# Two-layer RWKV-7 / short-convolution trunk: the triangular inverse of a chunk, in blocks of 48 or of 24

## The chip, the cores and the metric

The kernel runs on one core of one Trainium2 chip. The metric is device time in microseconds (us), from the first to the last instruction of the program with the little that lies around it; lower is better. One launch does the whole step: a prompt of 512 positions with 16 meta tokens ahead of it (528 positions), and 8 sample positions, 536 columns in all.

## The reference, cut to what matters

Each of the two layers is a half-step feed-forward block (FFN), a mixer, and a second half-step FFN. The mixer projects the normalised input, and its costly part is the RWKV-7 recurrence, for each of 16 heads of 64 channels, over the 528 prompt positions:

```
def _wkv_step(S, inp):
    r_t, w_t, k_t, v_t, a_t, b_t = inp
    Sa = jnp.einsum('bhvk,bhk->bhv', S, a_t)
    S = S * w_t[:, :, None, :] + Sa[..., None] * b_t[:, :, None, :] + v_t[..., None] * k_t[:, :, None, :]
    y = jnp.einsum('bhvk,bhk->bhv', S, r_t)
    return S, y
...
    seq_in = tuple(jnp.moveaxis(t, 1, 0) for t in (rh, wh, kh, vh, -kk, kk * ah))
    S_T, y = lax.scan(_wkv_step, wkv0.astype(f32), seq_in)
```

The state S of a head is updated with its own product with a_t, so the positions of a chunk depend on each other through a triangular system. The rest of the mixer is a group norm of y, a bonus term, a short convolution, two sigmoid gates and the product with W_o.

## The kernel before, in words

**Mixer.** The 16 heads go in 8 pairs p, two heads of 64 channels side by side on 128 partitions. The 528 positions are cut into NC = 11 chunks of C = 48. For each pair there are four pieces of code, all in the function `mixer`:

- `stage_k(p)` projects k and r, builds decay products, and fills `BK` and `mv` (operands whose products, `wg` on TensorE, are the 48x48 matrices of a chunk, for two heads 96x96 rows and columns). Its masked strictly triangular part is the tile `GT`, the other part `GR`. Then comes the inverse, (1 - G)^-1 of each chunk and head, 22 small triangular matrices of 48x48 for a pair.
- `stage_v(p)` projects v and makes `P1`, what a chunk contributes without the state.
- `chain(p)` runs through the 11 chunks in order. Each chunk takes the state `sd`, and goes TensorE (`cq<-mv,sd`), VectorE (`rh`), TensorE (transpose), VectorE (`rd`), TensorE with the inverse as weights (`cq<-rd,Yd`), ScalarE (`ud`), TensorE (`cq<-GR,ud`), VectorE (`sx`), TensorE (transpose), VectorE (`sd`). `cq` is one bank of PSUM, tag `c0` or `c1` by p % 2.
- `gnorm(p)` normalises the outputs of the pair, on the same bank.

Between them `fill` puts parts of the convolution and gate work (`gated_parts`), which depend on nothing in the chain. `sample()`, near the end of a mixer, does the recurrence for the 8 sample positions, with a good part of its elementwise work on GpSimd.

**The inverse.** `GT` is stored to DRAM (`td<-GT`), and read back so that each of 88 partitions holds a matrix: 22 matrices, four times (`Ta` its first 24 rows, `Tb` the rest). Partition group q works on the rows j of X with j % 4 = q. X starts as the identity (`Xinv<-in_xid`, a DMA). Then 47 steps, column by column: a product (`pr<-Ta,Xinv`) and an addition (`Xinv<-Xinv,pr`), both on GpSimd, since no pair is listed in `inv`. X is stored (`xd<-Xinv`, four DMAs), and read back in the layout of TensorE's weights (`Yd<-xd`, two DMAs), into one of two buffers `yds[p % 2]`. `Xinv`, `Ta`, `Tb` and `pr` have one buffer each.

**What sets the order.** Nothing is issued as it is written. `Sched.add` records every operation (so all instructions have the line of `issue`, L268, and are told apart by their tiles), and `flush` replays them as a list scheduler: it takes the operation that is ready and has the best priority (`prio`, its place less `boost`; the table `MIX` has the boosts by kind of work), and advances its own clocks by `price`. Each engine then runs its instructions strictly in that order, and so does the one DMA queue, SyncE's. The prices thus fix the order; how long things take is the chip's matter. The table `MIX`, with the fills in `gated`, is the same in both kernels. Small operations of GpSimd (`NS`, `SGA`, `GSs`, `MBs`, `CVP`, `pe`, copies of a few columns) stand in its order between the steps of the inverse; some of them are the last readers of tiles that other engines then write anew.

In `price`, times are in us and n is the number of elements of a partition:

```
return (max(n, 256) / 2400 + (12e-3 if self.ffn else 2.3e-3) if ins[0].dtype == F32R else n / 600 + 6e-3), self.HOP
...
last = any(tuple(x.ap[-1])[0] == 0 for x in ins)
return 0.155 + n * (1.63e-3 if last else 2.07e-3), self.HOP
```

The first is TensorE's, the last two GpSimd's, in a mixer. Matrix products in a mixer are mostly `acc`, projections in three fp32r products of 268 columns a block (`hi` and `lo` are the weights split by ScalarE and VectorE, from `raw`, the weights as loaded by SyncE's queue).

Of the kernel before, what the change touches and what calls it, by code (L numbers as in the profile page):

```python
# [15 lines left out]
P = 128  # L16
# [16 lines left out]
NC = L // C  # L33
D = 64
# [62 lines left out]
class Sched:  # L97
# [41 lines left out]
    def price(self, eng, fn, out, ins, kw):  # L139
        n = self.width(out)  # L140
        if fn == "dma_start":
            return 0.48, 4 * n * out.shape[0] / self.DMA_RATE
        if eng == "tensor":
            if fn == "transpose" or kw.get("is_transpose"):
                return n / 1200 + 2e-3, self.HOP
            return (max(n, 256) / 2400 + (12e-3 if self.ffn else 2.3e-3) if ins[0].dtype == F32R else n / 600 + 6e-3), self.HOP
        if eng == "vector":
            if fn == "memset":
                return 8e-3 + n / 960, self.HOP
            if fn == "reciprocal":  # L150
# [3 lines left out]
            return (0.13 if len(ins) > 2 else 0.07) + n / 960, self.HOP  # L154
        if eng == "scalar":
            psum = any(x.tensor.space == PSUM for x in ins + [out])
            return (0.05 if psum else 0.095) + (0.09 if "scale" in kw else 0) + n / 1200, self.HOP
        if self.ffn:
            return 0.1 + n * 3.1e-3, self.HOP
        last = any(tuple(x.ap[-1])[0] == 0 for x in ins)  # L160
        return 0.155 + n * (1.63e-3 if last else 2.07e-3), self.HOP

    def add(self, eng, fn, args, kw):
# [7 lines left out]
        if eng == "tensor":  # L171
            o.cols0 = (o.cost - 2.3e-3) * 2400
            o.cols = o.cols0 * ins[0].shape[0] / 128
# [165 lines left out]
def v2(ap):  # L339
    return ap.rearrange("p (a b) -> p a b", a=2)  # L340

# [5 lines left out]
class Build:  # L347
# [425 lines left out]
    def mixer(self, l, xh, xl, mD):  # L773
# [8 lines left out]
        with ExitStack() as ctx:  # L782
# [86 lines left out]
            def shift(i, acc, out, sample=None, dup=False):  # L869
                ps = tmp("ps_")  # L870
                V.memset(ps[:, 0:1], 0.0)
                evict(ps[:, 1:1 + NT], acc)
                G.tensor_copy(out=NS[:, i, :], in_=ps[:, L:L + 1 + NB])
                t = tmp("t_")
                n = NT if sample is not None else L
                A.activation(out=t[:, :n], in_=ps[:, 1:1 + n], func=AF.Copy, scale=omu[:, i:i + 1])
                pv, tv = ps[:, 0:L], t[:, :L]
                if dup:
                    pv, tv = c3(pv), c3(tv)
# [43 lines left out]
            def stage_k(p):  # L923
# [58 lines left out]
                for h in range(2):  # L982
                    hs = slice(h * D, (h + 1) * D)
                    V.scalar_tensor_tensor(out=BK[hs, :, h * C:(h + 1) * C], in0=c3(ka[hs, :L]), scalar=pc("kk", p)[hs],
                                           in1=c3(rn[hs, :L]), op0=ALU.mult, op1=ALU.mult)
# [30 lines left out]
                HC = C // 2  # L1016
                Ta = pp.tile([P, HC, C], F32, tag="Ta", name="Ta")
                Tb = pp.tile([P, HC, HC], F32, name="Tb")
                tdv = td.rearrange("h c s t -> (h c) s t")
                for q in range(4):  # L1020
                    S.dma_start(out=Ta[q * 22:(q + 1) * 22], in_=tdv[:, :HC, :])
                    S.dma_start(out=Tb[q * 22:(q + 1) * 22], in_=tdv[:, HC:, HC:])
                NP = 88
                nc.boost = boost['i']
                X = pp.tile([P, C // 4, C], F32, name="Xinv")
                pr = pp.tile([P, 176], F32, name="pr")
                I = V if p in opt['inv'] else G
                S.dma_start(out=X[:NP].rearrange("p j t -> p (j t)"), in_=io["xid"])
                for st in range(C - 1):
                    nj, nt = st // 4 + 1, C - 1 - st  # L1030
                    tr = Ta[:NP, st, st + 1:] if st < HC else Tb[:NP, st - HC, st - HC + 1:]
                    pv = pr[:NP, :nj * nt].rearrange("p (j t) -> p j t", j=nj)
                    I.tensor_tensor(out=pv, in0=tr.unsqueeze(1).to_broadcast([NP, nj, nt]),
                                    in1=X[:NP, :nj, st:st + 1].to_broadcast([NP, nj, nt]), op=ALU.mult)
                    I.tensor_tensor(out=X[:NP, :nj, st + 1:], in0=X[:NP, :nj, st + 1:], in1=pv, op=ALU.add)
                xd = dd.tile([2, NC, C, C], F32, tag="xd", name="xd")
                for q in range(4):
# [22 lines left out]
            def stage_v(p):  # L1060
# [3 lines left out]
                for h in range(2):  # L1064
                    hs = slice(h * D, (h + 1) * D)
                    V.tensor_copy(out=BK[hs, :, h * C:(h + 1) * C], in_=c3(s["kt"][hs, :]))
                v = pp.tile([P, NC, 2, C], F32, name="v")
# [4 lines left out]
                for cs in PCS:  # L1072
                    n = len(cs)
                    w = psp.tile([P, 512], F32, tag="wk", name="wv")
                    for i, c in enumerate(cs):
                        T.transpose(w[:2 * C, i * P:(i + 1) * P], v[:, c].rearrange("p a t -> p (a t)"), cst["id"])
# [15 lines left out]
                E('bv').tensor_tensor(out=c3(bv), in0=c3(s["rs"]), in1=v[:, :, 0, :], op=ALU.mult)  # L1092
                s["bv"] = bv

            def chain(p):
# [5 lines left out]
                for c in range(NC):  # L1101
                    o1, o2, o3 = order(c)
                    cq = psp.tile([P, 512], F32, tag=tg, name="cq", bufs=1)
                    rh = pp.tile([P, 2, C], F32, tag="rh", name="rh", bufs=2)
                    pb = P1[:, c, o1:o1 + C].unsqueeze(1).to_broadcast([P, 2, C])
                    if sd is not None:
                        T.matmul(out=cq[:, :QW], lhsT=sd, rhs=mvc(mv, c), start=True, stop=True)
                        V.tensor_tensor(out=rh, in0=cq[:, o1:o1 + C].unsqueeze(1).to_broadcast([P, 2, C]), in1=pb, op=ALU.add)
# [4 lines left out]
                    T.matmul(ct[:2 * C, 0:P], rh.rearrange("p a t -> p (a t)"), cst["id"], is_transpose=True, **gc)  # L1113
# [122 lines left out]
            def sample():  # L1236
# [233 lines left out]
def _consts():  # L1470
# [11 lines left out]
    s = np.arange(P) % C  # L1482
# [5 lines left out]
    o["mv"] = ((np.arange(P) // C)[:, None] == hb[None]).astype(f)  # L1488
# [4 lines left out]
def _xid():  # L1493
    import numpy as np
    x = np.zeros((88, C // 4, C), np.float32)
    for p in range(88):
        for j in range(C // 4):
            x[p, j, 4 * j + p // 22] = 1
# [82 lines left out]
```

## Time and profile before

| what | value |
|---|---|
| median of 3 runs | 3038.67 us (3034.83 to 3040.36) |
| the profiled execution | 3028.59 us, span 3026.8 us |
| mean granted TensorE clock | 0.973 |
| TensorE busy | 2835.8 us, 94% of the span |
| VectorE, ScalarE, GpSimd busy | 2170.7, 1337.4, 1043.2 us |
| GpSimd in the steps of the inverse | 402.0 + 200.0 + 166.0 us |

The first mixer lies from about 394 to 1115 us of the span, the second from 1893 to 2615; the rest is FFN, and there GpSimd is all but idle. In the rows of the profile, "idle before" is the time for which an engine stood still ahead of an instruction, and the arrow names what ended the wait. A matrix product of fp32 operands is two MATMUL instructions, one of fp32r or a transpose is one. TensorE's granted clock is 1.0 or 0.5 in stretches of 3.41 us.

### The profile page before, as it was taken

To read this page: it belongs to the slowest core of one execution; us is meant where nothing else is said; L and a number is where in the kernel's file an instruction comes from. 1 tells how busy PE (TensorE), PEld (TensorE's weight loads), DVE (VectorE), ACT (ScalarE), POOL (GpSimd) and SP (SyncE) were. 2 spreads that over 40 slices of the span, in tenths; PEclk is the share of its full clock that TensorE was granted. 3 is DMA by queue.
4 is the path that set the end of the run, shared out by engine and by line. 5 is a ranking of instruction groups with operands and counts; after the bars stand their busy time and mean duration, and the time that the engine had idled before them with its cause. 6 is when DMAs were issued, how large, how long until landed. Compare 5 with 4: busy or idle time off the path is not lost. (4 is left out here: it accounts for less than half of the span.)

```text
span 3026.8 us, 56336 instructions
## 1 busy us (share of the span) xinstructions
PE 2835.8 (94%) x22146; PEld 2782.0 (92%) x22146; DVE 2170.7 (72%) x3995; ACT 1337.4 (44%) x2190; POOL 1043.2 (34%) x1886
## 2 busy tenths in 40 slices
PE   8999998988997899999999999999898988899997
PEld 8999998988897889999999999888888888899997
DVE  8777676766775868776687776766777659687774
ACT  5444453433443345444444444534444332554444
POOL 1000037776777811000100001477877778100001
PEclk9999999999999999999999999999999999999999
DMA  4233333223323462333323323332233133623232
GB/s 134 90 102 98 116 97 83 69 84 89 94 63 91 149 199 91 96 97 102 108 77 92 102 89 126 89 82 72 82 97 94 46 113 130 209 88 98 95 105 78
DMA packets 203802, 303.88 MB, mean 100 GB/s; under 512 B 102704, under 2 KB 110256, under 8 KB 203536
## 3 DMA queue, kind: packets, MB, share of 16 engines
q1 hardware_dynamic: 203536, 300.27, 32.7%
q8 instruction: 174, 2.85, 0.4%
q14 instruction: 92, 0.75, 0.1%
HBM read 264.49 MB, written 35.72 MB: 99 GB/s over the span
## 5 line engine op out<-in xcount | busy, mean ns | idle before, releaser
L268 ACT ACTIVATE hi<-raw 128x1024 fp32r<-128x1024 f32 (+4 forms) x460 | 387.4, 845 | 498.3 <-PE acc L268 188.9
L268 DVE TENSOR_TENSOR lo<-raw,hi 128x1024 fp32r<-128x1024 f32 (+4 forms) x460 | 461.0, 1004 | 78.6 <-ACT hi L268 71.8
L268 PE MATMUL acc<-xh,lo 128*128 128x268 f32 (+1 forms) x2112 | 484.5, 303 | 15.6 <-DVE lo L268 15.4
L268 PE MATMUL acc<-xh,hi 128*128 128x268 f32 (+1 forms) x2112 | 484.9, 304 | 11.4 <-ACT hi L268 4.8
L268 PE MATMUL acc<-xl,hi 128*128 128x268 f32 (+1 forms) x2112 | 482.3, 301 | 0.0
L268 POOL MEMSET wide<- 128x104 f32 (+1 forms) x7 | 1.3, 188 | 1328.7 <-DVE lo L268 1264.1
L268 POOL TENSOR_TENSOR Xinv<-Xinv,pr 88x140 f32<-88x140 f32 (+36 forms) x752 | 402.0, 535 | 54.8
L268 PEld LDWEIGHTS acc<-xh,lo 128*128 128x128 f32 x2112 | 350.2, 195 | 19.7 <-DVE lo L268 19.4
L268 PEld LDWEIGHTS acc<-xh,hi 128*128 128x128 f32 x2112 | 350.8, 195 | 16.8 <-ACT hi L268 8.3
L268 PEld LDWEIGHTS acc<-xl,hi 128*128 128x128 f32 x2112 | 348.4, 195 | 0.2
L268 PE MATMUL a<-hh,lo 128*128 128x268 f32 (+1 forms) x1408 | 287.6, 286 | 0.2 <-DVE lo L268 0.2
L268 PE MATMUL a<-hl,hi 128*128 128x268 f32 (+1 forms) x1408 | 287.2, 285 | 0.0
L268 PE MATMUL a<-hh,hi 128*128 128x268 f32 (+1 forms) x1408 | 286.5, 285 | 0.0
L268 POOL TENSOR_TENSOR pr<-Ta,Xinv 88x150 f32<-88x150 f32 (+21 forms) x384 | 200.0, 521 | 147.9 <-DMA Xinv<-in_xid 57.5
L268 PE MATMUL x<-xh,hi 128*128 128x268 f32 (+1 forms) x864 | 247.1, 286 | 1.6 <-ACT sn L268 1.6
L268 PE MATMUL x<-xl,hi 128*128 128x268 f32 (+1 forms) x864 | 247.0, 286 | 0.0
L268 PE MATMUL x<-xh,lo 128*128 128x268 f32 (+1 forms) x864 | 246.8, 286 | 0.0
L268 ACT ACTIVATE hi<-s 128x1024 fp32r<-128x1024 f32 x144 | 151.3, 1057 | 177.1 <-DVE s L268 101.3
L268 PEld LDWEIGHTS a<-hh,lo 128*128 128x128 f32 x1408 | 219.3, 188 | 0.5 <-DVE lo L268 0.4
L268 PEld LDWEIGHTS a<-hl,hi 128*128 128x128 f32 x1408 | 218.6, 188 | 0.0
L268 PEld LDWEIGHTS a<-hh,hi 128*128 128x128 f32 x1408 | 218.5, 188 | 0.0
L268 DVE TENSOR_TENSOR lo<-s,hi 128x1024 fp32r<-128x1024 f32 x144 | 173.4, 1221 | 16.5 <-ACT hi L268 15.7
(562 smaller groups left out, 7235.2 us busy)
## 6 DMA issues: line engine op xcount, KB each, us to landing
raw<-in_f_in SPq DMA_DIRECT2D x176, 512.0 KB
raw<-in_w_in SPq DMA_DIRECT2D x132, 512.0 KB
raw<-in_f_out SPq DMA_DIRECT2D x128, 256.0 KB
raw<-in_f_out SPq DMA_DIRECT2D x32, 384.0 KB
raw<-in_w_o SPq DMA_DIRECT2D x32, 256.0 KB
Ta<-td SPq DMA_DIRECT2D x64, 99.0 KB
XD<-X SPq DMA_DIRECT2D x16, 268.0 KB
s<-in_swkv SPq DMA_DIRECT2D x16, 256.0 KB
```

The costliest lines, as they stand in the source:

```text
L268: return getattr(getattr(self.nc, o.eng), o.fn)(*o.args, **o.kw)
```

## The change

The 48x48 matrix of a chunk and head is taken as two diagonal blocks of HC = 24 and one block off the diagonal. GpSimd inverts only the diagonal blocks, 44 of 24x24 for a pair: 88 partitions hold 44 matrices twice, group q does the rows with j % 2 = q, and there are 23 steps. The block off the diagonal is the product of the lower inverse, the block itself and the upper inverse, made on TensorE, in two groups of 6 and 5 chunks: a transpose (`w1`), a product (`w2`), a product (`w3`), each followed by a copy out of PSUM on ScalarE (`x1`, `x2`, and into `Yd`). They use the chain's bank `c{p % 2}`. The rows of a chunk for the two heads are interleaved by blocks (head 0 and 1 of the first half, then of the second), so the views of `BK`, `v`, `rh`, the masks and `mv` change with it (`g3` where `c3` stood), with the same numbers of elements. `Ta` and `Xinv` have two buffers; `Tb` is gone.

```
-            return (max(n, 256) / 2400 + (12e-3 if self.ffn else 2.3e-3) if ins[0].dtype == F32R else n / 600 + 6e-3), self.HOP
+            return (max(n, 256) / 2400 + 12e-3 if ins[0].dtype == F32R else n / 600 + 6e-3), self.HOP
...
+            if not self.ffn and len(ins) > 1 and all(x.tensor.space != PSUM for x in ins):
+                return fixed + n / 860, self.HOP
...
-        last = any(tuple(x.ap[-1])[0] == 0 for x in ins)
-        return 0.155 + n * (1.63e-3 if last else 2.07e-3), self.HOP
+        return 0.2 + n * 3e-3, self.HOP
...
-                td = dd.tile([2, NC, C, C], F32, tag="td", name="td")
-                for h in range(2):
-                    S.dma_start(out=td[h].rearrange("c s t -> s c t"), in_=GT[h * C:(h + 1) * C, :, :])
...
+                td = dd.tile([4, NC, HC, C], F32, tag="td", name="td")
+                for g in range(4):
+                    S.dma_start(out=td[g].rearrange("c s t -> s c t"), in_=GT[g * HC:(g + 1) * HC])
+                NP, HJ = 88, HC // 2
+                Ta = pp.tile([P, HC, HC], F32, tag="Ta", name="Ta", bufs=2)
...
+                X = pp.tile([P, HJ, HC], F32, tag="Xinv", name="Xinv", bufs=2)
+                pr = pp.tile([P, HJ * HJ], F32, name="pr")
...
-                for st in range(C - 1):
-                    nj, nt = st // 4 + 1, C - 1 - st
-                    tr = Ta[:NP, st, st + 1:] if st < HC else Tb[:NP, st - HC, st - HC + 1:]
+                for st in range(HC - 1):
+                    nj, nt = st // 2 + 1, HC - 1 - st
...
-                for q in range(4):
-                    S.dma_start(out=xd.rearrange("h c (j q) t -> q (h c) j t", q=4)[q], in_=X[q * 22:(q + 1) * 22])
+                for q in range(2):
+                    S.dma_start(out=xd.rearrange("g c (j q) t -> q (g c) j t", q=2)[q], in_=X[q * 44:(q + 1) * 44])
+                Yd = yds[p % 2]
+                for g in range(4):
+                    rw = slice(g * HC, (g + 1) * HC)
+                    S.dma_start(out=Yd[rw, :, rw], in_=xd[g].rearrange("c j t -> j c t"))
                 for h in range(2):
-                    S.dma_start(out=yds[p % 2][h * C:(h + 1) * C, :, h * C:(h + 1) * C], in_=xd[h].rearrange("c j t -> j c t"))
+                    rw = slice(h * HC, (h + 1) * HC)
+                    S.dma_start(out=off[rw, :, rw], in_=td[h, :, :, HC:].rearrange("c s t -> s c t"))
+                    S.dma_start(out=Yd[rw, :, C + h * HC:C + (h + 1) * HC], in_=xd[2 + h].rearrange("c j t -> j c t"))
+
+                for c0, c1 in SPL:
+                    n = c1 - c0
...
+                    def step(fn, out, name):
+                        w = psp.tile([P, 512], F32, tag=f"c{p % 2}", name=name, bufs=1)
+                        for i in range(n):
+                            fn(w[:C, i * C:(i + 1) * C], c0 + i)
+                        A.activation(out=out, in_=w[:C, :n * C].rearrange("p (c q) -> p c q", c=n), func=AF.Copy)
+
+                    step(lambda o, c: T.transpose(o, Yd[:C, c, :C], cst["id"][:C, :C]), x1, "w1")
+                    step(lambda o, c: T.matmul(out=o, lhsT=off[:C, c, :], rhs=x1[:, c - c0, :], start=True, stop=True), x2, "w2")
+                    step(lambda o, c: T.matmul(out=o, lhsT=x2[:, c - c0, :], rhs=Yd[:C, c, C:], start=True, stop=True),
+                         Yd[:C, c0:c1, C:], "w3")
```

What the scheduler makes of it, at three places of the first mixer (the line is L268 before and L271 in the change; the number behind a tile's name is its instance). First, SyncE's queue where the inverse of pair 3 is stored. Before, `Xinv_5209` is that pair's, and the `raw` loads are weights of projections and of the fills; `Tb_5395` belongs to pair 4:

```order
L268 DMA Tb_5395<-td_5393 22x24x24
L268 DMA xd_5211<-Xinv_5209 264x1x48
L268 DMA Tb_5395<-td_5393 22x24x24 x3
L268 DMA raw_5581<-in_w_in 128x1024
L268 DMA raw_5556<-in_w_in 128x1024
L268 DMA xd_5211<-Xinv_5209 264x1x48
L268 DMA gsD_77<-ta_5421 128x528
L268 DMA xd_5211<-Xinv_5209 264x1x48
```

In the change the same pair's X is `Xinv_5236`:

```order
L271 DMA mb_5293<-mbD_76 128x528
L271 DMA xd_5238<-Xinv_5236 528x1x24 x2
L271 DMA Yd1_4736<-xd_5238 24x11x24 x4
L271 DMA Xinv_5616<-in_xid 88x288
L271 DMA Yd1_4736<-xd_5238 24x11x24 x2
L271 DMA raw_5406<-in_w_in 128x1024
L271 DMA raw_5390<-in_w_in 128x1024
```

Loads of weights stand behind the store of X in both. Before, the read of the next pair's `Tb` stands ahead of the store and waits for the end of the same inverse; in the change that read is gone, two stores are left of four, and six reads of `Yd` take the place of two. The X that is loaded there, `Xinv_5616`, is that of pair 5, two pairs ahead; before, the load after the stores of pair 3 is that of pair 4, into the same buffer.

Second, GpSimd at the end of pair 3's inverse and the beginning of pair 4's. Before:

```order
L268 TENSOR_TENSOR pr_5210<-Tb_5208,Xinv_5209 88x12
L268 TENSOR_TENSOR Xinv_5209<-Xinv_5209,pr_5210 88x12
L268 COPY GSs_4729<-ta_5421 128x8
L268 COPY NS_4723<-ps__5536 128x9
L268 COPY SGA_4728<-sig_5542 128x8
L268 COPY SGA_4728<-a_5544 128x8
L268 TENSOR_TENSOR pr_5397<-Ta_5394,Xinv_5396 88x47
```

In the change:

```order
L271 TENSOR_TENSOR pr_5237<-Ta_5235,Xinv_5236 88x12
L271 TENSOR_TENSOR Xinv_5236<-Xinv_5236,pr_5237 88x12
L271 COPY GSs_4729<-ta_5266 128x8
L271 COPY NS_4723<-ps__5381 128x9
L271 COPY SGA_4728<-sig_5387 128x8
L271 COPY SGA_4728<-a_5389 128x8
L271 COPY pe_5397<-pm_5396 128x11
L271 COPY NS_4723<-ps__5410 128x9
L271 TENSOR_TENSOR pr_5433<-Ta_5431,Xinv_5432 88x23
```

The copies stand behind the last step of an inverse in both. The inverse ahead of them has 94 instructions before and 46 in the change, and before the next one follows at once. In the change more copies (`pe`, a second `NS`) stand between two inverses.

Third, TensorE in the chain of pair 2 (`cq` with `Yd0`). Before:

```order
L268 MATMUL cq_5276<-cst_69,rh_5277 96x128
L268 MATMUL acc_5415<-xh_775,hi_5413 128x268 x2
L268 MATMUL acc_5415<-xl_776,hi_5413 128x268 x2
L268 MATMUL acc_5415<-xh_775,lo_5414 128x268 x2
L268 MATMUL acc_5415<-xh_777,hi_5413 128x268
L268 MATMUL wp_5431<-G2_5430,Vd_5428 128x160
L268 MATMUL cq_5276<-rd_5278,Yd0_4735 96x128
```

In the change, with the products for pair 3 (`Yd1`) in the same chain:

```order
L271 MATMUL w1_5241<-cst_69,Yd1_4736 48x48 x5
L271 MATMUL cq_5307<-cst_69,sx_5311 128x128
L271 MATMUL acc_5380<-xl_784,hi_5378 128x268 x2
L271 MATMUL acc_5380<-xh_783,lo_5379 128x268 x2
L271 MATMUL acc_5380<-xh_785,hi_5378 128x268 x2
L271 MATMUL w2_5242<-x1_5239,off_4737 48x48 x6
L271 MATMUL cq_5313<-mv2_4733,sd_5312 128x160
L271 MATMUL acc_5380<-xl_786,hi_5378 128x268 x2
L271 MATMUL acc_5380<-xh_785,lo_5379 128x268 x2
L271 MATMUL acc_5380<-xh_787,hi_5378 128x268
L271 MATMUL w3_5243<-Yd1_4736,x2_5240 48x48 x6
```

The three steps are set between the steps of another pair's chain, with five or six instructions of a projection between one step and the next, and some eight chunks ahead of the chain that uses them.

More of the change, by code (lines that the diff above doesn't have):

```diff
@@ L33 @@
 NC = L // C
+HC = C // 2
 D = 64
@@ L171, in add @@
         if eng == "tensor":
-            o.cols0 = (o.cost - 2.3e-3) * 2400
+            o.cols0 = (o.cost - 12e-3) * 2400
             o.cols = o.cols0 * ins[0].shape[0] / 128
@@ L340, in v2, with g3 @@
     return ap.rearrange("p (a b) -> p a b", a=2)
+def g3(ap):
+    return ap.rearrange("p (g t) -> p g t", g=2 * NC)
 def c3(ap):
@@ L848, in mixer @@
                 yds.append(t)
+            off = pp.tile([P, NC, C], F32, name="off")
+            G.memset(off, 0.0)
             def mname(c):
@@ L1024, in stage_k @@
+                Ta = pp.tile([P, HC, HC], F32, tag="Ta", name="Ta", bufs=2)
+                for q in range(2):
+                    for b in range(2):
+                        o = (2 * q + b) * 22
+                        S.dma_start(out=Ta[o:o + 22], in_=td[2 * b:2 * b + 2, :, :, b * HC:(b + 1) * HC].rearrange("h c s t -> (h c) s t"))
                 nc.boost = boost['i']
-                X = pp.tile([P, C // 4, C], F32, name="Xinv")
-                pr = pp.tile([P, 176], F32, name="pr")
+                X = pp.tile([P, HJ, HC], F32, tag="Xinv", name="Xinv", bufs=2)
@@ new lines, in stage_k @@
+                for q in range(2):
+                    S.dma_start(out=xd.rearrange("g c (j q) t -> q (g c) j t", q=2)[q], in_=X[q * 44:(q + 1) * 44])
[3 more added lines that the diff above has]
+                    S.dma_start(out=Yd[rw, :, rw], in_=xd[g].rearrange("c j t -> j c t"))
+                for h in range(2):
+                    rw = slice(h * HC, (h + 1) * HC)
+                    S.dma_start(out=off[rw, :, rw], in_=td[h, :, :, HC:].rearrange("c s t -> s c t"))
+                    S.dma_start(out=Yd[rw, :, C + h * HC:C + (h + 1) * HC], in_=xd[2 + h].rearrange("c j t -> j c t"))
@@ L1075, in stage_v @@
                     for i, c in enumerate(cs):
-                        T.transpose(w[:2 * C, i * P:(i + 1) * P], v[:, c].rearrange("p a t -> p (a t)"), cst["id"])
+                        T.transpose(w[:2 * C, i * P:(i + 1) * P], v[:, 2 * c:2 * c + 2].rearrange("p b a t -> p (b a t)"), cst["id"])
                     Vd = pp.tile([P, 3, P], F32, tag="Vd", name="Vd", bufs=2)
@@ L1091, in stage_v @@
                 bv = pp.tile([P, L], F32, tag="bv", name="bv", bufs=2)
-                E('bv').tensor_tensor(out=c3(bv), in0=c3(s["rs"]), in1=v[:, :, 0, :], op=ALU.mult)
+                E('bv').tensor_tensor(out=g3(bv), in0=g3(s["rs"]), in1=v[:, :, 0, :], op=ALU.mult)
                 s["bv"] = bv
@@ L1112, in chain @@
                     ct = cq[:, QW:]
-                    T.matmul(ct[:2 * C, 0:P], rh.rearrange("p a t -> p (a t)"), cst["id"], is_transpose=True, **gc)
+                    T.matmul(ct[:2 * C, 0:P], rh.rearrange("p b a t -> p (b a t)"), cst["id"], is_transpose=True, **gc)
                     gc["start"] = False
@@ L1494, in _xid @@
     import numpy as np
-    x = np.zeros((88, C // 4, C), np.float32)
+    x = np.zeros((88, HC // 2, HC), np.float32)
     for p in range(88):
-        for j in range(C // 4):
-            x[p, j, 4 * j + p // 22] = 1
+        for j in range(HC // 2):
+            x[p, j, 2 * j + p // 44] = 1
     return x.reshape(88, -1)
```

47 lines of the change are left out of this document (22 added, 25 removed).

## The prediction

> **What bounds the kernel now.** I read the page's totals, then the table by stretches (FFN, mixer, FFN, mixer, FFN). Its columns are length, busy time of TensorE, its weight loads, VectorE, ScalarE, GpSimd, each with its instructions, then the granted clock, DMA share and rate; here are a mixer, the FFN between, and the other mixer.
>
> ```profile
> span 3026.8 us, 56336 instructions
> PE 2835.8 (94%) x22146; PEld 2782.0 (92%) x22146; DVE 2170.7 (72%) x3995; ACT 1337.4 (44%) x2190; POOL 1043.2 (34%) x1886
> ...
> 394.00:1115.00 721.00, 642.30 (x4865) 623.05 (x4864) 515.11 (x1154) 297.94 (x532) 480.24 (x907) 0.96 0.34 98
> 1115.00:1893.00 778.00, 772.18 (x6201) 768.80 (x6200) 563.03 (x842) 365.06 (x552) 27.81 (x21) 1.00 0.32 101
> 1893.00:2615.00 722.00, 648.41 (x4867) 623.91 (x4866) 517.63 (x1138) 301.56 (x537) 494.67 (x923) 0.95 0.33 97
> ```
>
> TensorE bounds the FFN, which the change leaves alone. There an instruction costs 778.0 / 6201 = 0.1255 us. At that rate a mixer's 4865 would need 611 us; the mixers take 721 and 722. So they lose about 222 us together, 152 of them as idle TensorE (721.0 - 642.3 and 722.0 - 648.4), the rest mostly at half clock. The next rows are the first and last of 22 stretches at half clock inside the mixers, and their sum; the two numbers are length and TensorE's busy time.
>
> ```profile
> 439.00:442.40 3.40, 2.92 (x13) 0.50 1.04 144
> ...
> 2510.90:2514.30 3.40, 3.40 (x17) 0.50 0.37 125
> sum 133.00, PE 96.03; mean PE 4.37
> ```
>
> What 96.0 us did at half clock would take half: 48 us. Next, what makes TensorE wait. The groups of GpSimd, and the first and last instructions of the first inverse with the first of the second:
>
> ```profile
> L268 POOL TENSOR_TENSOR Xinv<-Xinv,pr 88x140 f32<-88x140 f32 (+36 forms) x752 | 402.0, 535 | 54.8
> 443.77 0.26 POOL L268 TENSOR_TENSOR pr<-Ta,Xinv 88x47 f32<-88x47 f32 x1 [4.30 <-DMA raw<-in_w_in]
> ...
> 501.49 0.22 POOL L268 TENSOR_TENSOR Xinv<-Xinv,pr 88x12 f32<-88x12 f32 x1
> 514.52 0.26 POOL L268 TENSOR_TENSOR pr<-Ta,Xinv 88x47 f32<-88x47 f32 x1 [12.56 <-DMA Xinv<-in_xid]
> ```
>
> An inverse takes 501.71 - 443.77 = 57.9 us, and the next can't start until the one X is stored and refilled (12.56 us idle). The scheduler's prices for its 94 instructions add up to 33.2 us (5044 elements in each kind of 47, at 1.63 and 2.07 ns, and 0.155 us each). So the order that all engines follow is written for an inverse that is 24.7 us shorter than the real one. What waits behind it in order comes late. One such place is the longest idle time of TensorE in a mixer; the rows are TensorE, ScalarE, SyncE's queue and GpSimd.
>
> ```profile
> 719.71 0.80 PE L268 MATMUL cq<-GR,ud 96*128 96x128 f32 x2 [9.54 <-ACT ud L268]
> 718.44 1.06 ACT L268 ACTIVATE hi<-raw 128x1024 fp32r<-128x1024 f32 x1 [14.31 <-DMA raw<-in_w_in]
> 710.73 0.84 SPq L268 DMA_DIRECT2D xd<-Xinv  x1
> 713.26 0.38 SPq L268 DMA_DIRECT2D raw<-in_w_in  x1
> 710.37 0.21 POOL L268 TENSOR_TENSOR Xinv<-Xinv,pr 88x12 f32<-88x12 f32 x1
> ```
>
> The queue stands before the store of X until 710.6; the weights behind it are issued at 713.26, ScalarE waits 14.3 us for them with `ud` behind, and the chain and all projections stop. I followed every TensorE gap over 1.2 us in the mixers back like this through the timeline. Nineteen lead to GpSimd's inverse, through SyncE's queue or through a small copy that stands behind the inverse; they add up to 80 us. The other seven of the largest:
>
> ```profile
> 927.13 1.12 PE L268 MATMUL wg<-mv,BK 128*96 128x160 f32 x3 [7.91 <-ACT P L268]
> 974.25 0.48 PE L268 MATMUL cq<-cst,sx 128*128 128x128 f32 x1 [7.70 <-DVE P L268]
> 2476.53 0.62 PE L268 MATMUL ws<-cst,V 128*48 128x128 f32 x2 [5.79 <-DVE V L268]
> 787.86 0.81 PE L268 MATMUL wn<-kql,cr 128*128 128x264 f32 x2 [5.46 <-DVE kql L268]
> 495.57 0.81 PE L268 MATMUL wn<-kqh,cr 128*128 128x264 f32 x2 [4.96 <-ACT kqh L268]
> 2014.83 0.71 PE L268 MATMUL cq<-rd,Yd 96*96 96x128 f32 x2 [4.41 <-DMA Yd<-xd]
> 2129.34 0.74 PE L268 MATMUL cq<-rd,Yd 96*96 96x128 f32 x2 [4.40 <-DVE rd L268]
> ```
>
> With the 9.54 these make 50 us; eleven more of 1.6 to 4.6 us make 30. Fifteen of the 22 half-clock stretches follow these gaps; in them TensorE is busy for 66.8 us, a loss of 33. So 113 of the 222 us lead back to the inverse. A second witness are the queue's own waits and the chain of waits from 2286 us to the second mixer's end (329 us).
>
> ```profile
> SPq L268 <- POOL pr L268: 139.2, 16, 18.8
> SPq L268 <- POOL Xinv L268: 133.1, 13, 22.8
> by line: PE acc L268 21.4%; POOL Xinv L268 13.5%; POOL pr L268 11.9%; issue 10.1%; PE cq L268 5.4%; POOL t L268 3.1%; DVE lo L268 3.0%; DVE s L268 2.1%; PE wg L268 1.6%; DVE sm L268 1.6%; DVE z L268 1.5%; PE wp L268 1.4%; DMA mbD<-z 1.3%; S
> ```
>
> A quarter of that chain, 84 us, is on the inverse's steps.
>
> **The change, part by part.** *GpSimd.* 23 steps in place of 47, on 53 elements in the mean (1222 / 23). The nearest rows:
>
> ```profile
> L268 POOL TENSOR_TENSOR pr<-Tb,Xinv 88x55 f32<-88x55 f32 x16 | 7.9, 493 | 1.1
> L268 POOL TENSOR_TENSOR Xinv<-Xinv,pr 88x55 f32<-88x55 f32 x16 | 5.2, 326 | 1.2
> ```
>
> A step is 0.493 + 0.326 us with 0.07 idle ahead of each (1.1 / 16), 0.96 us; an inverse 22 us. By the mean step of before (57.9 / 47) it would be 28. The new price (0.2 us and 3 ns an element) gives 16.5 in the order, so 5.5 us are left of an overrun of 24.7. I let the stalls shrink in proportion: 113 x (24.7 - 5.5) / 24.7 = 88 us less. At 28 us an inverse it is 60 us less, and all 113 if 5.5 us always fit in the slack. The wait for X's refill (12.56 us) goes with the second buffer, and is in these stalls already.
>
> *TensorE.* For each of 16 pairs and 11 chunks a transpose and two fp32 products, five instructions: 880. No row has 48x48. The nearest are eight transposes of 8x8 in a run, each with a weight load of its own, and ten fp32 products of one column:
>
> ```profile
> 1075.23 0.66 PE L268 MATMUL ws<-cst,yb 8*128 8x8 f32 x8
> L268 PE MATMUL ws<-cst,yb x16: 200/201/225, 1075.2 to 2579.7; 8*128 8x8 f32 x16
> 3010.96 1.28 PE L268 MATMUL ss<-cst,wide 128*128 128x1 f32 x10 [2.33 <-DVE wide L268]
> ```
>
> The first gives (0.66 - 0.20) / 7 = 0.066 us from one to the next, 58 us for 880; the second 0.128, 113 us. With 48 columns on each side the first is nearer. Lying in what idle time remains, they would cost nothing. I take 55 on the path, between 0 and 113.
>
> *New waits.* TensorE now waits in order for the reads of `Yd` (16 times) and for ScalarE's copies between steps (96 times). The like of before, over 16 reads and 176 chunks:
>
> ```profile
> PE cq L268 <- DMA Yd<-xd: 6.9, 2, 4.4
> PE cq L268 <- ACT ud L268: 18.5, 7, 9.5
> ```
>
> That is 6.9 us for 16 and 0.105 for each of 96: 17 us. Below it could be nothing, since other pairs' work stands between the steps in the order; above, see the second rival. What is queued behind a step that waits is the running chain and the projections.
>
> *ScalarE* gets 96 copies of 288 or 240 columns, like these:
>
> ```profile
> L268 ACT ACTIVATE yc<-wm 128x288 f32<-128x288 f32 x16 | 6.5, 404 | 28.2 <-PE wm L268 28.1
> L268 ACT ACTIVATE yc<-wm 128x240 f32<-128x240 f32 x16 | 5.8, 366 | 7.0 <-PE wm L268 7.0
> ```
>
> 48 x (0.404 + 0.366) = 37 us beside 843 us in which ScalarE is idle in the mixers: hidden, and where the cover fails it is the wait just priced. *SyncE's queue* issues 19 DMAs a pair for 17:
>
> ```profile
> L268 SPq DMA_DIRECT2D xd<-Xinv x64: 807/838/1342, 501.8 to 2500.7; - x64
> L268 SPq DMA_DIRECT2D Yd<-xd x32: 308/408/676, 510.0 to 2503.5; - x32
> ```
>
> Two stores of 0.84 us less and six block reads (four `Yd`, two `off`) of 0.41 more; with a second pair of `td` and half as many reads of `Ta` and `Tb`, 0.3 us more a pair, 2 if a store of 528 rows costs twice one of 264. It is hidden behind the 90 us that a pair lasts. From the last step to `Yd` the queue's own time stays about equal.
>
> *The other prices* only move work. An fp32r product was planned 9.7 ns too short, about 31 us over the 3168 `acc` products of a mixer, and now is planned at the measured pace. No row prices that; the gain lies between nothing and the 109 us of loss that remain. I take a quarter, 27, since the chain's ten hops a chunk stay whatever the order.
>
> Sum: -88 + 55 + 17 - 27 = -43 us. The profiled execution took 3028.6, so 2986 for the like; the median of the runs is 10.1 us above it, so I forecast 2996.
>
> **The rivals.** *A, the mixers become TensorE's:* with the inverse out of the way half of the remaining 109 us goes too, and all 113: -113 - 55 + 55 = -113, 2926. For it speaks the chain of waits; against it that TensorE also waits for `P`, `rd` and `lo` of VectorE, 72% busy.
>
> *B, slower: the three steps hold TensorE.* Each needs a copy that stands in ScalarE's order behind a `hi` of 1.06 us (row at 718.44). Without new waits the sum is -60, so it decides at 60 / 96 = 0.63 us a step. At 1.06 it is +42: 3081. Against it: 7 of 176 like waits; for it: 96 steps, each planned with less than 1 us of other products ahead of the next.
>
> *C, the clock.* Each group of small products could bring a half-clock stretch: 16 of 6.8 us, with 96.03 / 133 of it busy and half of that lost, 39 us, so -4 and 3035, no change. Before such a stretch TensorE is sparse; this is the one ahead of that at 2391.4:
>
> ```profile
> 2388.00:2391.40 3.40, 2.30 (x10) 1.00 0.31 60
> ```
>
> Against it, the order sets the small products among full ones. The Trainium skill, "TensorE: Matmul & The Clock Gate", Part 4, says that transposes don't count as a busy TensorE to the clock gate; by that rule the time would be C's, 3035, against 2996 by the rows. The trace has no run of transposes alone that would show it.
>
> **How the numbers follow.** The forecast gets 0.61, A 0.13, B 0.18, C 0.08. The forecast's own range is 2948 to 3044, from 60 to 113 us of stalls, 0 to 113 of TensorE, 0 to 40 of waits, 0 to 55 by order, not all at one end. The range reaches to A, 2926, and nearly to B, 3078, with a tenth outside at each end. A measurement tells about 0.2%, 6 us, from no change. The forecast is faster in 0.84 of its cases and slower in 0.09; with A, B and half of C: faster 0.68, same 0.06, slower 0.26.
>
> **What would show it.** Right: inverses of 20 to 28 us; GpSimd's busy time in a mixer near 200 us; the queue's waits for `Xinv` and `pr` at a third of 272 us or less; mixers of about 700 us with idle TensorE near 100 for both. Wrong: TensorE waiting for ScalarE ahead of `w2` and `w3` for more than 0.6 us each (B); half-clock stretches behind `w1` to `w3` (C); `w` products at 0.11 us or more; or stalls as before that lead to another engine, which would make the inverse their place and not their cause.

## The result, and the profile after

The changed kernel takes 3000.74 us (median of 4 runs, 2998.38 to 3002.65) against 3037.99 for the kernel before (4 runs, 3034.83 to 3040.36). The ratio is 0.9878, 95% interval 0.9861 to 0.9895: 37 us less, where 42.7 were forecast. The profiled execution took 2998.38 us with a span of 2996.6.

Span and totals of the page of the changed kernel, and its answers for the two stretches that the prediction took as the mixers (columns as there):

```profile
span 2996.6 us, 57546 instructions
PE 2873.9 (96%) x23026; PEld 2807.0 (94%) x23026; DVE 2134.4 (71%) x3995; ACT 1360.5 (45%) x2278; POOL 572.8 (19%) x1120
...
394.00:1115.00 721.00, 678.24 (x5368) 648.24 (x5367) 509.06 (x1162) 313.89 (x584) 242.76 (x525) 0.98 0.32 93
1893.00:2615.00 722.00, 674.65 (x5389) 644.22 (x5388) 504.28 (x1144) 316.61 (x589) 260.97 (x533) 0.98 0.33 97
```

GpSimd does a little more than half of what it did (572.8 us of 1043.2), and TensorE has 880 instructions more, yet stands idle for 90 us in these stretches where it was 152. The stretches at half clock, asked for as before (the first, the last and the sum of eleven rows):

```profile
447.00:450.40 3.40, 3.40 (x17) 3.40 (x16) 3.40 (x7) 2.62 (x4) 3.17 (x6) 0.51 0.50 161
...
2546.10:2570.00 23.90, 8.62 (x37) 7.59 (x38) 13.27 (x27) 10.46 (x28) 2.04 (x3) 0.50 0.65 204
sum 68.10, PE 48.12 PEld 44.06 DVE 44.53 ACT 23.74 POOL 13.33; mean PE 4.37 PEld 4.01 DVE 4.05 ACT 2.16 POOL 1.21
```

They are half as long as before (133.00 us with 96.03 busy). The inverse, by its groups on GpSimd, the queue's only long wait for it, and the chain of waits in the second mixer:

```profile
L271 POOL TENSOR_TENSOR Xinv<-Xinv,pr 88x22 f32<-88x22 f32 (+16 forms) x368 | 143.8, 391 | 26.1
L271 POOL TENSOR_TENSOR pr<-Ta,Xinv 88x22 f32<-88x22 f32 (+16 forms) x368 | 135.8, 369 | 161.5 <-DMA Ta<-td 136.3
...
SPq L271 <- POOL Xinv L271: 57.3, 11, 10.1
...
by line: PE acc L271 42.8%; PE cq L271 9.5%; PE wg L271 5.5%; PE w L271 3.8%; PE wp L271 3.4%; issue 3.4%; DVE lo L271 2.8%; POOL Xinv L271 1.6%; POOL pr L271 1.5%; DMA raw<-in_w_o 1.5%; PE wv L271 1.4%; ACT hi L271 1.4%; DMA Yd<-xd 1.2%; D
```

From the first step to the last an inverse takes 19.2 to 28.3 us, 23.2 in the mean of 16 (56.8 before). GpSimd now waits 136.3 us for the next matrices. The inverse holds 3% of this chain (1.6 + 1.5), where it held a quarter of the chain that ended the kernel before's second mixer. At the end of pair 3's inverse (629 us now), where TensorE waited 9.54 us before, nothing is left: from 514 to 885 us TensorE has no wait over 1.2 us.

To place gains and losses, each trace is split in three. Idle is the span less TensorE's busy time; half clock is half of TensorE's busy time in the windows at 0.5; work is the rest, TensorE's busy time as it would be at full clock. Ratios are to the kernel before, with 95% intervals; all in us.

| kernel | ratio | span | idle | half clock | work |
|---|---|---|---|---|---|
| before | 1 | 3026.8 | 191.0 | 55.6 | 2780.3 |
| the change | 0.9878 (0.9861 to 0.9895) | 2996.6 | 122.7 | 29.7 | 2844.2 |
| e1 blocks, old prices | 0.9975 (0.9962 to 0.9989) | 3030.2 | 144.0 | 43.9 | 2842.2 |
| e2 48, new prices | 1.0387 (1.0367 to 1.0406) | 3155.2 | 279.7 | 76.1 | 2799.3 |
| e3 no merge | 0.9629 (0.9613 to 0.9645) | 2923.2 | 116.0 | 32.6 | 2774.6 |
| e4 merge twice | 0.9966 (0.9949 to 0.9983) | 3020.7 | 105.5 | 32.7 | 2882.5 |
| e5 48, true price | 1.0806 (1.0779 to 1.0833) | 3282.7 | 369.7 | 107.7 | 2805.2 |
| e6 old GpSimd price | 0.9967 (0.9953 to 0.9981) | 3025.7 | 135.9 | 49.7 | 2840.2 |
| e7 old TensorE price | 0.9956 (0.9942 to 0.9970) | 3029.2 | 137.3 | 51.0 | 2840.9 |
| e8 one X, one Ta | 1.0063 (1.0041 to 1.0084) | 3047.6 | 181.7 | 31.1 | 2834.8 |
| e9 one X | 0.9922 (0.9896 to 0.9947) | 3012.4 | 135.7 | 36.7 | 2840.0 |
| e10 slow inverse | 1.0252 (1.0219 to 1.0285) | 3106.8 | 192.6 | 77.8 | 2836.4 |
| e11 48, copies moved | 0.9989 (0.9974 to 1.0003) | 3037.3 | 192.5 | 67.5 | 2777.3 |
| e12 ScalarE's price | 0.9948 (0.9934 to 0.9962) | 3013.7 | 139.2 | 38.6 | 2835.9 |

So the change takes 68 us of idle time and 26 of half clock away, 94 together, and adds 64 us of work: 30 us less by the spans of the two profiled executions, 37 by the medians.

### The profile page after: what moved, and what is told of

The parts are those of the page before. It is cut to its first block, busy times and chain, and to the rows that moved or that the text cites. A ratio compares the mean times of both kernels' runs of the same rounds, so it can differ in the third digit from the quotient of the medians.

```text
span 2996.6 us, 57546 instructions
## 1 busy us (share of the span) xinstructions
PE 2873.9 (96%) x23026; PEld 2807.0 (94%) x23026; DVE 2134.4 (71%) x3995; ACT 1360.5 (45%) x2278; POOL 572.8 (19%) x1120
## 4 chain that ended last, share of the span: by engine, by line
PE 63%; DVE 8%; DMA 5%; ACT 2%; POOL 2%; issue 2%; SPq 1%; DVEq 0%; ACTq 0%; POOLq 0%
PE acc L271 20%; PE a L271 12%; PE x L271 9%; PE cq L271 4%; PE y L271 4%; DVE lo L271 2%; PE wg L271 2%; PE au L271 2%; PE ag L271 2%; PE z L271 2%; DMA raw<-in_f_in 2%; PE w L271 2%; PE wp L271 1%; ACT hi L271 1%; POOL pr L271 1%
## 5 line engine op out<-in xcount | busy, mean ns | idle before, releaser
L271 ACT ACTIVATE hi<-raw 128x1024 fp32r<-128x1024 f32 (+4 forms) x460 | 388.0, 845 | 484.6 <-PE acc L271 181.2
L271 DVE TENSOR_TENSOR lo<-raw,hi 128x1024 fp32r<-128x1024 f32 (+4 forms) x460 | 451.7, 983 | 54.3 <-ACT hi L271 47.7
L271 PE MATMUL acc<-xh,lo 128*128 128x268 f32 (+1 forms) x2112 | 480.8, 300 | 8.9 <-DVE lo L271 8.8
L271 PE MATMUL acc<-xh,hi 128*128 128x268 f32 (+1 forms) x2112 | 478.9, 300 | 9.4 <-ACT hi L271 3.7
L271 PE MATMUL acc<-xl,hi 128*128 128x268 f32 (+1 forms) x2112 | 481.4, 299 | 0.0
L271 PEld LDWEIGHTS acc<-xh,hi 128*128 128x128 f32 x2112 | 341.7, 191 | 16.3 <-ACT hi L271 6.9
L271 PEld LDWEIGHTS acc<-xh,lo 128*128 128x128 f32 x2112 | 342.8, 191 | 13.7 <-DVE lo L271 12.3
L271 PEld LDWEIGHTS acc<-xl,hi 128*128 128x128 f32 x2112 | 343.5, 191 | 1.0
L271 PE MATMUL a<-hh,lo 128*128 128x268 f32 (+1 forms) x1408 | 287.3, 285 | 0.0
L271 PE MATMUL a<-hl,hi 128*128 128x268 f32 (+1 forms) x1408 | 287.3, 285 | 0.0
L271 PE MATMUL a<-hh,hi 128*128 128x268 f32 (+1 forms) x1408 | 287.1, 285 | 0.0
L271 POOL MEMSET wide<- 128x104 f32 (+1 forms) x7 | 1.3, 188 | 1338.4 <-DVE lo L271 1261.8
L271 PE MATMUL x<-xh,hi 128*128 128x268 f32 (+1 forms) x864 | 246.6, 286 | 0.8 <-ACT sn L271 0.8
L271 PE MATMUL x<-xl,hi 128*128 128x268 f32 (+1 forms) x864 | 246.7, 286 | 0.0
L271 PE MATMUL x<-xh,lo 128*128 128x268 f32 (+1 forms) x864 | 246.3, 285 | 0.0
L271 ACT ACTIVATE hi<-s 128x1024 fp32r<-128x1024 f32 x144 | 152.0, 1057 | 171.0 <-DVE s L271 121.5
L271 PEld LDWEIGHTS a<-hh,lo 128*128 128x128 f32 x1408 | 219.4, 188 | 0.0
L271 PEld LDWEIGHTS a<-hh,hi 128*128 128x128 f32 x1408 | 218.8, 188 | 0.0
L271 PEld LDWEIGHTS a<-hl,hi 128*128 128x128 f32 x1408 | 218.6, 188 | 0.0
L271 DVE TENSOR_TENSOR lo<-s,hi 128x1024 fp32r<-128x1024 f32 x144 | 173.3, 1220 | 17.1 <-ACT hi L271 16.6
L271 POOL TENSOR_TENSOR pr<-Ta,Xinv 88x22 f32<-88x22 f32 (+16 forms) x368 | 135.8, 369 | 161.5 <-DMA Ta<-td 136.3
L271 DVE SCALAR_TENSOR_TENSOR X<-a,X 128x536 f32<-128x536 f32 (+1 forms) x160 | 113.1, 707 | 74.5 <-PE a L271 74.4
```

The costliest lines, as they stand in the source:

```text
L271: return getattr(getattr(self.nc, o.eng), o.fn)(*o.args, **o.kw)
```

## The experiments

Two theories stood at the start. O, the prediction's: TensorE stalls because the inverse lasts longer than the order allows for. L: the inverse's length and its single buffers matter, whatever it is planned at. Two more, B and P, come with the last runs, and are told in their expectations.

**What the merge costs (e3, e4).** e3 removes the three steps, e4 issues each of their products twice.

```
-                for c0, c1 in SPL:  ... step(..., "w1"); step(..., "w2"); step(..., "w3")      (e3)
-                        for i in range(n):                                                     (e4)
+                        for i in list(range(n)) * 2:
                             fn(w[:C, i * C:(i + 1) * C], c0 + i)
```

> The changed kernel without the three merge steps (no w1, w2, w3 and none of their 96 copies; the block off the diagonal stays what the DMAs left, so the output is not the reference's; the DMAs stay). By the prediction's terms -55 for 880 instructions and -17 for waits: 2929. If the products lie in time in which TensorE would be idle anyway (90 us in both mixers): 2990 to 3001.

> The changed kernel with each of the 880 instructions of the merge issued twice into the same place (same result, no new waits, no new copies). If TensorE's work is on the path: +54 (the products take 54.2 us from start to start in the trace of the changed kernel), 3055. If it lies in idle time: 3001 to 3015.

Without the merge it is 2925.70 us, 0.9878 - 0.9629 = 2.5% or 76 us less than the change: 70 of it work, 7 idle, and 3 the other way at half clock. A second set of the products costs 0.9%, 27 us: 38 of work (43 ns each), of which 17 come out of idle time. So the second set is partly hidden; the first is not, and the time without the merge is close to the expected 2929. Of the 76 us the idle time is only 7, although TensorE waits 17 us for the merge's operands: without the merge it stands idle elsewhere. The waits of the merge, in the changed kernel:

```profile
PE w L271 <- DMA Yd<-xd: 12.1, 9, 2.9
PE w L271 <- POOL Xinv L271: 4.8, 1, 4.8
L271 PE MATMUL w<-x,off x352: 205/205/241, 483.3 to 2426.8; 48*48 48x48 f32 x176
L271 PE MATMUL w<-cst,Yd x176: 199/203/278, 477.9 to 2425.3; 48*48 48x48 f32 x176
```

TensorE waits 17.2 us in all ahead of `w1` (12.1 + 4.8 and one wait of 0.2), for the inverse to arrive, and not once ahead of `w2` or `w3` (75 groups of them): the copies on ScalarE are always in time.

**Prices or blocks (e1, e6, e7, e12).** e1 gives the change all three old prices, e6 only GpSimd's, e7 only TensorE's; e12 makes ScalarE's price truer.

```
+        last = any(tuple(x.ap[-1])[0] == 0 for x in ins)                            (e1, e6)
+        return 0.155 + n * (1.63e-3 if last else 2.07e-3), self.HOP
+            return (max(n, 256) / 2400 + (12e-3 if self.ffn else 2.3e-3) ...        (e1, e7)
+            return (0.05 if psum else 0.095) + ... + (0 if self.ffn else 0.08) ...  (e12)
```

> The changed kernel with the prices of before (TensorE, VectorE, GpSimd). Theory O (overrun): stalls come from an inverse that lasts longer than its price. The old price plans the 23 steps at 46 x 0.155 + 1222 x 3.7 ns = 11.7 us against 23.2 measured, an overrun of 11.5 us where the new price leaves 6.7; at 113 / 24.7 = 4.6 us of stalls for each us of overrun that is +22, and +27 for TensorE's price: 3050. Theory L (length): what counts is that the inverse is short and has two buffers, so its price hardly matters: 3000 to 3010. If TensorE's price alone matters: 3028.

> The changed kernel with GpSimd's price of before alone. It plans the inverse at 11.7 + 4.6 (hops) = 16.3 us against 23.2 measured, where the new price with its hops plans 21.1. Theory O: 113 us for the 14 us that the inverse of before overran its plan makes 8 us for each us, so 4.8 us more of overrun cost 38: 3039. If the 30 us between the changed kernel and the one with all old prices come from TensorE's price: 3001.

> The changed kernel with TensorE's price of before alone (an fp32r product in a mixer planned 9.7 ns shorter). The prediction's term: +27, 3028. If GpSimd's price is what counts: 3001.

> The changed kernel with ScalarE's price in the mixers 0.08 us higher (a copy of `ud` is planned at 0.157 us and takes 0.27 in the trace of the changed kernel, a `hi` of 1024 columns is planned at 0.948 and takes 1.06). If each price nearer to the chip makes the order better, as TensorE's and GpSimd's did for 25 us each: half of that or more, ratio to before 0.980 to 0.984, 2980 to 2990. If the order now is as good as prices make it, since TensorE is idle for only 90 us in both mixers: ratio 0.986 to 0.990, about 3001.

With old prices the blocks still gain, 0.25%, about 8 us; with the new ones 1.2%. By the table e1 has 59 us less idle time and half clock than the kernel before, and 62 us more work: the blocks alone hardly more than pay for their merge, and most of the change's gain comes with the prices. GpSimd's price alone is worth 0.9%, 27 us, TensorE's alone 0.8%, 24 us, and both with VectorE's only 29 us: they don't add up, so each is a different order, not a share of one fault. The short price of GpSimd does what theory O says, in part: TensorE's waits ahead of `w1` grow from 17 us to 29 (e6) and 37 (e1). The larger part of the loss in e6 and e7 is clock, 20 and 21 us of the table's half-clock column; 5 and 14 of these lie in windows of a kind that the change doesn't have, and that the last section shows. And a truer price for ScalarE made the kernel slower by 0.7%, 21 us, where one theory expected 11 to 21 us less and the other no change. Both missed, and why this order is worse was not traced. That a price is nearer to the chip is no guarantee that the order is better.

**Is it the overrun (e2, e5)?** e2 gives the kernel before the new prices; e5 gives it those of TensorE and VectorE, and for the inverse the measured price:

```
+        return 0.306 + n * 2.64e-3, self.HOP
-            ("scalar", "scalar"): 0.15, ("gpsimd", "gpsimd"): 0.1}
+            ("scalar", "scalar"): 0.15, ("gpsimd", "gpsimd"): 0.0}
```

> The kernel before (47 steps, one buffer, no merge) with the three new prices alone. They plan the inverse at 94 x 0.2 + 10088 x 3 ns = 49.1 us against 56.8 measured, an overrun of 7.7 us for 23.6. Theory O: the stalls go from 113 to 113 x 7.7 / 23.6 = 37 us, -76, and -27 by TensorE's price: 3038 - 103 = 2935, faster than the change itself. Theory L: the inverse is as long as before and each pair still takes 57 us and 12 us of refill, so at most the 27 us of TensorE's price: 3011 or more.

> The kernel before (47 steps, one buffer) with the change's prices of TensorE and VectorE, and a step of the inverse at 0.306 us and 2.64 ns an element as measured in the trace of before, with no hop of 0.1 us from GpSimd to itself, so that in the plan nothing slips between two steps: the inverse is planned at 55.4 us against 56.8 measured. (The prices of before with that hop plan 33.2 + 9.4 = 42.6 us, those of the run with 48 and new prices 58.5.) Theory O (overrun): all 113 us of stalls go, and 27 by TensorE's price: 2900. Theory L (length): eight inverses of 57 us with 12.6 of refill follow one another from 444 us on, so the last ends no earlier than 991 us for 999 before, and what follows it takes 126 us: at most 16 us less in both mixers, 3020; more where the plan lets other work between.

Theory O expected 103 us less in e2, theory L at most 27 less, and it took 118 more; e5 took 243 more, where they expected 138 less (2900) and 18 less (3020). (With the hop of 0.1 us that the next section explains, e2's plan of the inverse is 58.5 us, not the 49.1 of its expectation, so it has no overrun either.) With 48 columns a truthful plan is worse. In e2 the scheduler sees room between two steps, and puts the sample step's additions there; the timeline of GpSimd near the end of the last inverse of the first mixer, and TensorE's longest wait in total:

```profile
1022.87 0.47 POOL L270 TENSOR_TENSOR Xinv<-Xinv,pr 88x152 f32<-88x152 f32 x1
1031.74 1.67 POOL L270 TENSOR_TENSOR t<-s,VB 128x512 f32<-128x512 f32 x1 [8.40 <-DVE s L270]
1033.38 0.43 POOL L270 TENSOR_TENSOR pr<-Tb,Xinv 88x144 f32<-88x144 f32 x1
...
PE cq L270 <- DMA Yd<-xd: 107.2, 6, 51.2
```

Between two steps GpSimd waits 8.40 us for VectorE. This inverse lasts 119 us and its like in the second mixer 121, about 60 too long each. TensorE waits for `Yd`, the result, 107.2 us in all, where it waited 6.9 before; two of these waits, 48 and 51 us, stand behind the two long inverses, and they are most of the loss. In e5 nothing can slip between, an inverse takes 51 us, and all small copies stand behind it (no other instruction of GpSimd lies inside any of its 16 inverses):

```profile
583.85 0.21 POOL L270 TENSOR_TENSOR Xinv<-Xinv,pr 88x12 f32<-88x12 f32 x1
584.01 0.19 POOL L270 COPY NS<-ps__5164 128x9 f32<-128x9 f32 x1
584.14 0.19 POOL L270 COPY SGA<-sig 128x8 f32<-128x8 f32 x1
584.23 0.71 ACT L270 ACTIVATE a<-acc,par 128x536 f32<-128x536 f32 x1 [21.10 <-POOL NS L270]
...
585.93 0.59 PE L270 MATMUL acc<-xh,hi 128*128 128x268 f32 x1 [20.74 <-ACT hi L270]
```

`NS` waits for the last step, ScalarE 21.10 us for `NS`, and TensorE 20.74 us for the `hi` that stands behind that instruction in ScalarE's order. The overrun is gone, yet TensorE is idle for 369.7 us. Theory O falls as the one cause.

**Which property of the long inverse (e8, e9, e10, e11)?** e8 and e9 take second buffers away, e10 makes the inverse long again and keeps the blocks, buffers and merge, e11 moves the small copies of the kernel before to VectorE:

```
-                Ta = pp.tile([P, HC, HC], F32, tag="Ta", name="Ta", bufs=2)              (e8)
-                X = pp.tile([P, HJ, HC], F32, tag="Xinv", name="Xinv", bufs=2)           (e8, e9)
+                    for _ in range(4):                                                   (e10)
                         I.tensor_tensor(out=pv, in0=Ta[...], in1=X[...], op=ALU.mult)
-                G.tensor_copy(out=NS[:, i, :], in_=ps[:, L:L + 1 + NB])                  (e11, and eight like it)
+                V.tensor_copy(out=NS[:, i, :], in_=ps[:, L:L + 1 + NB])
```

> The changed kernel with one buffer in place of two for X and for Ta. Pairs follow each other at about 72 us in the changed kernel, and an inverse of 23 with a refill of 13 takes half of that, so by theory L the second buffer is worth nothing now: 2996 to 3008. If the second buffer is what made the room: as far as 12.6 us for each of 14 later pairs, 3100 and more, or some part of that.

> The changed kernel with one buffer for X, Ta with two. In the run with one buffer for both, TensorE's 54 us of new idle time were two waits of 30 and 36 us at the end of the mixers, in the sample step, whose tile s2 shares Ta's tag; the inverses came at the same times as in the changed kernel. So if the second buffer of X is worth nothing at 23 us an inverse: 3001, within 8. If the inverse needs it: 3015 or more.

> The changed kernel with the product of each step issued four times in place of once (into the same pr, same result): five instructions a step, an inverse of 115 x 0.295 + 18.3 = 52 us at the measured pace, nearly that of the kernel before (56.8), planned at 46. Blocks, merge, two buffers and prices stay. Theory B (GpSimd as a block: during a long inverse the small copies behind it in order, and what waits for the result, come late): most of the 94 us that the change took off come back, 3070 to 3100. Theory P (pace: before, one X and one Ta made each pair take 70 us; with two buffers 52 us are shorter than the 72 between pairs, so the length does not matter): 3001 to 3015.

> The kernel before with the small operations of a pair (NS, SGA, pe, CVP, CVS, MBs, GSs, and the addition to z) on VectorE in place of GpSimd; inverse, prices and buffers as before. Eight of the 19 gaps that lead back to the inverse go through NS, SGA or z: 27 us, with half clock behind them some 35. Theory B: 3003. Theory P (the pace of 70 us a pair sets the mixer's length, whichever wait shows it): the inverse gets only a few us shorter by what stood between its steps, 3020 to 3040.

e8 loses 1.9%, 56 us, but not through the inverse. Its longest waits of TensorE:

```profile
PE ws L271 <- DMA yb<-yd: 65.5, 2, 35.8
PE w L271 <- DMA Yd<-xd: 15.5, 6, 5.1
```

The 65.5 us are the sample step at the end of each mixer, whose tile `s2` has the tag of `Ta` (7.7 us in the change); the waits for the inverse are no longer than in the change. e9 gives `Ta` its second buffer back, and the wait of the sample step is 12.6 us. What is left is 0.44%, 13 us, for X's second buffer, at the near edge of the case that the inverse needs it; the two intervals all but touch (0.9895 and 0.9896). TensorE's waits ahead of `w1` grow by 3 us only, so how X's buffer costs is open.

e10 loses 3.7%, 114 us, against the change, with work as in the change: 70 us are idle time and 48 half clock. It brings back more than the 94 us that the change removed, and is slower than the 3070 to 3100 of theory B. Its inverses last 57.7 us in the mean (56.8 before), and its page and waits read like this:

```profile
PE 2914.2 (94%) x23026; PEld 2845.4 (92%) x23026; DVE 2135.3 (69%) x3995; ACT 1368.2 (44%) x2284; POOL 994.9 (32%) x2224
PE w L271 <- DMA Yd<-xd: 51.4, 11, 8.6
PE wn L271 <- DVE kql L271: 7.4, 4, 2.1
```

Theory P expected 3001 to 3015 here, since there are two buffers: the length costs without a single buffer too. GpSimd's time in the inverse is what costs, both through the result that comes late (51.4 us) and through copies behind it (`kql` waits, in the timeline, for `SGA`).

e11 says that the copies are not the place where it could be cured. They are off GpSimd, and the time is the same (0.9989, 0.9974 to 1.0003). Theory B expected 3003 and missed; the time lies in theory P's 3020 to 3040, and from one inverse to the next it is still 70 us. TensorE's idle time stays at 192.5 us, and the largest waits have moved:

```profile
518.04 0.82 PE L268 MATMUL wg<-mv,BK 128*96 128x160 f32 x2 [12.88 <-DVE GR L268]
794.14 0.58 PE L268 MATMUL cq<-GR,ud 96*128 96x128 f32 x1 [10.55 <-ACT ud L268]
SPq L268 <- POOL pr L268: 113.0, 14, 22.7
```

Both go back through `lo` or `hi` to weights (`raw`) that SyncE's queue issued late, behind its stores of X.

What stays open: e10's inverse also overran its plan (57.7 us against 46, where the change plans 21.1), and the longer plan gives another order, so it doesn't tell length alone from length with overrun. e5 has the length without the overrun and is worse still, but its order is another. A kernel with 48 columns and second buffers was not tried, so for the kernel before it is not shown how much of the loss is the pace of 70 us a pair that its single buffers set (theory P, which e11 bears out) and how much the length by itself (e10).

## Why the prediction was right, and where it was not

- **What bounds the mixers.** Right. 113 us of stalls were traced to the inverse; with it short, and the new prices, the waits go (idle -68, half clock -26; -47 and -12 at the old prices, e1), and with it made long again (e10) more than all of them return.
- **The stalls, -88.** The size held, the rule behind it did not. The sum of prices, 33.2 us, left out the hop of 0.1 us that the scheduler puts between two operations of GpSimd that depend on each other (`HOPS`). With it the plan was 42.6 us and the overrun 15, not 24.7; in the change the plan is 21.1 for 23.2 measured. And "in proportion to the overrun" is refuted by e5, where the overrun went and idle time and half clock together rose from 247 us to 477. By the table these two fell by 94 in the change, where -88, +17 and -27 make -98. Since the rule does not hold, that the size came out is in part luck.
- **TensorE's products, +55.** From start to start the 880 take 54.2 us, as forecast from the 8x8 transposes, though by another split: 0.066 us each was forecast, and it is 43 to 45 ns in a run and 133 to 135 at the end of one, 62 in the mean. All work grew by 64; the other 10 us are not placed. e3 shows it on the path, as chosen, not hidden.
- **New waits, +17.** The sum was right (17.2) by luck, since its split was wrong: 6.9 were for reads and 10 for copies, and all of it went to reads. Rival B, which needed 0.63 us a step, had 0 at `w2` and `w3`.
- **The order by TensorE's price, -27.** e7 gives 24. The quarter that was taken had no row behind it, so this is luck too. The reason, an order nearer to the chip's pace, is not shown: e12 went the other way, and the larger part of e7's loss is clock.
- **Rival A, 2926.** It left the mixers 55 us of loss; they still have 90 us idle and 24 at half clock (48.12 / 2). That its 2926 is the time of the kernel without the merge (e3) is chance.
- **Rival C, 3035.** In the change half clock fell instead of rising. Its mechanism exists all the same, see the last section.
- **What was to be seen.** Inverses of 20 to 28 us: 23.2. The queue's waits at a third of 272 us or less: 57.3, a fifth. Idle TensorE near 100 us: 90. Mixers of about 700 us: missed; from a mixer's first `acc` product to the first FFN product behind it they take 723 and 717 us, where it was 731 and 732, so they lose 23 of the 30 us. GpSimd near 200 us a mixer: missed, 243 and 261.

## What to carry to other kernels

A long block of dependent small instructions on an engine that runs strictly in order costs through whatever stands behind it, and curing one such wait (e11) or planning it truthfully (e2, e5) moves the loss or makes it larger; making the block shorter took it away, 59 us at the old prices and 94 with the new ones, at 62 to 64 us of new work on the engine that bounds the kernel. So the net gain hung on the order as much as on the block. A list scheduler's order is worth tens of microseconds either way, so a price change needs a run of its own: three prices nearer to the chip gave 24, 27 and -21 us here. When a second buffer seems to matter, see which tile of its tag waits: most of e8's 56 us belonged to the sample step, not to the inverse.

## What the runs showed of the clock

Not expected: TensorE can be busy without a gap and stay at half clock. A stretch of the run with TensorE's old price, in windows of 3.4 us (length, then busy time of TensorE, weight loads, VectorE, ScalarE, GpSimd, then the granted clock); the second block has the same windows for the merge's instructions alone:

```profile
889.00:892.40 3.40, 0.49 (x2) 0.30 (x2) 2.07 (x4) 1.48 (x2) 0.00 (x0) 1.00 0.77 183
...
899.20:902.60 3.40, 3.40 (x22) 3.06 (x22) 0.41 (x2) 0.54 (x2) 0.00 (x0) 0.50 0.29 80
902.60:906.00 3.40, 3.40 (x23) 2.78 (x22) 0.35 (x1) 0.58 (x2) 0.00 (x0) 0.50 0.00 0
...
909.50:912.90 3.40, 3.40 (x16) 3.40 (x16) 0.29 (x1) 0.59 (x2) 0.00 (x0) 0.50 0.00 0
912.90:916.30 3.40, 3.40 (x30) 3.40 (x29) 1.76 (x4) 1.06 (x1) 0.00 (x0) 1.00 0.02 5
```

```profile
899.20:902.60 3.40, 1.19 (x12) 1.03 (x12) 0.40 (x1) 0.50 0.29 80
902.60:906.00 3.40, 1.12 (x12) 0.92 (x13) 0.36 (x1) 0.50 0.00 0
...
909.50:912.90 3.40, 0.00 (x0) 0.00 (x0) 0.32 (x1) 0.50 0.00 0
```

A gap at 889 us brings half clock, as elsewhere. Then four windows follow in which TensorE is busy for all 3.40 us with 12 to 17 of the 48x48 products among full ones, and the clock stays at 0.50; the first window without any (909.5) is followed by 1.00. Over all fourteen traces, of 190 windows at half clock that were over 97% busy with none of these products 187 were followed by full clock; with eight or more it was 1 of 35.

The Trainium skill, "TensorE: Matmul & The Clock Gate", Part 1, says that full clock comes after one busy window of about 3.4 us: the 187 of 190 agree, the 1 of 35 do not, so what counts as busy there is not what the trace shows as busy. Part 4 of the page, which the prediction weighed, excepts transposes. Of the 35 windows 23 had eight or more of the products `w2` and `w3` and no `w1`, and 1 of these was followed by full clock: plain small products count little too. No run varied their rows, their columns or their fp32 alone, but the traces lean to the rows. Take of each product the time to the next one's start, weigh it by its rows over 128, and add this up over a window. In the 245 windows at half clock that were over 97% busy, one threshold, 0.84 of the window, then tells which were followed by full clock, but for 4. Weighed by the columns of the weights the best threshold fails in 18, and with fp32 products left out in 39, as many as if all were said to be followed; 11 windows that were mostly other, larger fp32 products were all followed by full clock. The scheduler's own model of the clock (`clocked` in the kernel) weighs a product's columns by its rows over 128 in the same way.

This is one way in which the order costs time with the same work: where the small products happen to follow a gap, half of TensorE's time in these windows is lost, 14 us in e7, 10 in e4 and 19 in e10, and nothing in the change. At full clock they do no harm: all 411 such windows of the nine runs with a merge were followed by full clock again. So rival C's gate is real, but it needs a gap ahead of it.
